# Two transpose banks in a two-layer transformer trunk: one allocation per task in place of alternating halves

## The chip, the core and the metric

The kernel runs on one core of one Trainium2 chip. The metric is the device time of one launch in microseconds (us). TensorE (PE) does the matrix products and the transposes, its weight load is listed apart (PEld), VectorE (DVE), ScalarE (ACT) and GpSimd (POOL) do the elementwise work, SyncE (SP) issues the weight transfers.

## The reference

The input x is (1, 256, 1024) in float32: 256 tokens of 1024 features. Two layers follow each other, each with a half-weighted SwiGLU block, a mixing block and a second half-weighted SwiGLU block:

```python
x = x + 0.5 * swiglu(rms_norm(x, norm_ffn1), w_gate, w_up, w_down)
xn = rms_norm(x, norm_mix)
q, k, v = split(xn @ w_in)                  # 16 heads of 64
x = x + concat(heads_1, heads_2) @ w_out
x = x + 0.5 * swiglu(rms_norm(x, norm_ffn2), w_gate, w_up, w_down)
```

In layer 0 eight heads are stick-breaking heads (a weight per key from log-sigmoids and a running sum over later keys) and eight are block-sparse heads, which with 256 tokens and blocks of 256 are plain causal softmax heads; their q and k get an RMS norm and a rotary embedding. In layer 1 eight heads are forgetting heads (causal softmax whose logits get a difference of cumulated log gates; q and k normed) and eight are dilated-window heads (softmax with fixed weights per distance; q and k normed and rotated).

## The kernel before

**Precision and weights.** Every large product is made of three matmuls with split operands (`mm3`, L153-156): hi by hi, hi by lo, lo by hi. The weights come from HBM through the SP queue into `raw` (3 buffers); ACT casts the hi part (L238), DVE subtracts to get the lo part (L239), 9 buffers for each. Tokens lie in two tiles t of 128. A product is either token-major (`token_major`, weights as the moving operand, 512 columns) or feature-major (`feature_major`, SwiGLU), eight contraction tiles each.

**PSUM.** Eight banks: three `acc` for projections, one `o` for attention outputs, two `z` for logits and for the up projection, and two banks `tt` (one tile of [128, 2, 512]) for transposes. `slot()` (L147) hands out the left and the right 256 columns of both `tt` banks in turn, so two users of `tt` that follow each other lie in different columns of the same two banks. Users of a slot: the transposes of the normed x (`Normed.transpose`, one per token tile and column half of 512), the product `ones x diag` that spreads 1/rms over the partitions (`inverse`), the transposes of the SwiGLU hidden tiles (`hidden`), those of normed or rotated q and k (`project_norm`), the small products of the forget gates (`forget`), the running sums of stick-breaking (`stick_b`, one per head) and the transposes of the softmax weights (`soft_b`, one per head).

**Order of the work.** The order of TensorE is written by the program itself: `Weave` (L70) keeps an estimated clock `pe.t`. A task (a generator) yields a lead; it is resumed, and its next TensorE instructions are put into the stream, at the first poll after that much estimated matmul time. The leads stand at the top: `LEAD_R0` 14 for the rotated q of the first group, `LEAD_R` 9 for its k, `LEAD_N` 6.5 for normed q and k without rotation, `LEAD_F` for the forget gates, `PACE` for the distance between the steps of a head group. The other engines' orders are made by a scheduler from the same program; each engine works through its own queue in that order.

**The mixing block.** The projections come in the order q2, k2, v2 (first group: causal softmax heads in layer 0, dilated heads in layer 1), then in layer 1 the forget gates, then q1, k1, v1 (second group: stick-breaking heads in layer 0, forgetting heads in layer 1), then the output rows of the first group (`out_rows`, 48 matmuls) and those of the second. A group has four pairs of heads. `Group.run` (L581) goes through steps i: `a_(i)` makes the logits of pair i in the two `z` banks and starts its softmax on ACT and DVE (or the log-sigmoids); `b_` transposes the weights of pair i-1 (or makes its running sums), and DVE (or, for stick, ACT through an exponential) brings them to `pT`; `c(i-2)` multiplies by v into `o`; after every second pair `out` splits `o` into `oh` and `ol`. Between the steps TensorE works on what the projections and output rows have left. The second group starts when the first has made four steps.

For rotated heads (`project_norm`) the chain between the projection and its transposes runs over ACT (squares), DVE (`hss`, mean), POOL (power -0.5, `rp`), DVE (`qn`, `qs`), and POOL also makes the products of gains and rotation tables `gc` and `gs` in between.

Of the kernel before, what the change touches and what calls it, by code (L numbers as in the profile page):

```python
# [8 lines left out]
F32 = mybir.dt.float32  # L9
# [7 lines left out]
P = 128  # L17
TAIL = 3
LEAD_R, LEAD_R0, LEAD_N, LEAD_F, OVER = 9.0, 14.0, 6.5, 8.0, 4
LEAD_X = ((1.7, 1.7), (1.7, 3.0))  # L20
LEAD_0 = 3.0
PACE = ((6.5, 6.0), (6.5, 6.0))
# [90 lines left out]
def trunk(ctx, tc, a, out):  # L113
# [30 lines left out]
    tt = psum.tile([P, 2, 512], F32, tag="tt", bufs=1, name="tt")  # L144
    slots = [0]

    def slot():  # L147

        slots[0] += 1
        c0 = (slots[0] % 2) * 256  # L150
        return tt[:, :, c0:c0 + 256]
# [11 lines left out]
    def transposes(src, n):  # L163

        tb = slot()
        for j in range(n):
            for b in range(2):
                r = slice(b * HP, (b + 1) * HP)
                nc.tensor.transpose(tb[:, b, j * HP:(j + 1) * HP], src[r, j * P:(j + 1) * P], ident[r, r])  # L169
            pe.t += 0.06  # L170
        return tb[:, :, :n * HP].rearrange("p b (c t) -> p c b t", t=HP)
# [87 lines left out]
    class Normed:  # L259
# [8 lines left out]
        def start(self, t, h, ps=None, scale=1.0, lead=None, gain=None):  # L268
            self.ready[t].append(pe.spawn(self.transpose(t, h, ps, scale, lead or LEAD_X[t][h], gain)))

        def transpose(self, t, h, ps, scale, lead, gain):
            tk, sl, kk = slice(t * P, (t + 1) * P), slice(h * 512, (h + 1) * 512), slice(4 * h, 4 * h + 4)
            if ps is not None:
                residual(ps, t, h, scale)
            xg = xpool.tile([P, 512], F32, tag="xg", bufs=2, name=nm("xg"))
            nc.vector.tensor_mul(xg, x[t][:, sl], self.g[:, sl] if gain is None else gain)
            self.xg[t].append(xg)
            yield lead
            split_evac(transposes(xg, 4), self.hi[:, kk, tk], self.lo[:, kk, tk])
            if h == 1:  # L280
                self.rdone[t] = pe.spawn(self.inverse(t, self.xg[t]))

        def inverse(self, t, junk):
            sq = small.tile([P, 2], F32, tag="sq", name=nm("sq"))
            for h in range(2):
                nc.scalar.activation(junk[h], x[t][:, h * 512:(h + 1) * 512], AF.Square, accum_out=sq[:, h:h + 1])
            ss = small.tile([P, 1], F32, tag="ss", name=nm("ss"))
            nc.vector.tensor_add(ss, sq[:, 0:1], sq[:, 1:2])
            self.r[t] = rpow(ss, D, 1)
            if self.rb is None:  # L290
                return
            diag = xpool.tile([P, P], F32, tag="diag", name=nm("diag"))
            nc.gpsimd.tensor_mul(diag, ident, self.r[t].to_broadcast([P, P]))
            yield 5.0
            tb = slot()[:, 0]
            mm(tb[:, :P], ones, diag, True)
            nc.scalar.copy(self.rb[:, t * P:(t + 1) * P], tb[:, :P])
# [65 lines left out]
    def ffn(layer, wg, wu, wd, xt, done, between=None):  # L363
        with tc.tile_pool(name=nm("ffn"), bufs=1) as fp:
# [19 lines left out]
            def hidden(hs, c0, n):  # L384
                ft, m = c0 // P, n // P
                vs = [transposes(h, m) for h in hs]
                for t, v in enumerate(vs):
                    split_evac(v, hh[:, ft:ft + m, t * P:(t + 1) * P], hl[:, ft:ft + m, t * P:(t + 1) * P])
# [54 lines left out]
    def _mix(mp, layer, xt, gains, done):  # L443
# [24 lines left out]
        def project_norm(c0, g, tag, lead=LEAD_R):  # L468
# [4 lines left out]
            def norm(t, ps):  # L473
# [8 lines left out]
                if rope:  # L482
# [6 lines left out]
                    yield lead  # L489
# [3 lines left out]
                nc.scalar.activation(halves(qT[:, :, t * P:(t + 1) * P]), transposes(o, 4), AF.Copy,  # L493
# [5 lines left out]
        def forget():  # L499
# [13 lines left out]
            ps = slot()[:, 0]  # L513
# [5 lines left out]
            def rest():  # L519
# [9 lines left out]
                tb = slot()[:, 0]  # L529
# [5 lines left out]
                tb = slot()[:, 0]  # L535
# [24 lines left out]
        class Group:  # L560
# [11 lines left out]
            def run(self, after, pace, other):  # L572
# [5 lines left out]
                for i in range(4 + 2):  # L578
                    if i < 4:
                        a_(i)  # L580
                    if 0 <= i - 1 < 4:  # L581
                        b_(2 * (i - 1))
                        b_(2 * (i - 1) + 1)
# [35 lines left out]
            def stick_b(self, h):  # L619
                sp, ls = self.z.pop(h)  # L620
                b = slot()
                mm(b[:, 0], cv("suf"), sp[:, 0:256], True)
                mm(b[:, 0, P:], cv("nones"), sp[:, 256:384], False)
                mm(b[:, 1, :P], cv("suf"), sp[:, 256:384], True)
                nc.vector.tensor_add(ls[:, 0:256], ls[:, 0:256], b[:, 0])
                nc.vector.tensor_add(ls[:, 256:], ls[:, 256:], b[:, 1, :P])
                pT = self.pT[h] = new("pT", 384, 4)
                nc.scalar.activation(pT, ls, AF.Exp)
# [37 lines left out]
            def soft_b(self, h):  # L666
                tb = transposes(self.z.pop(h), 3)
                pT = self.pT[h] = new("pT", 384, 4)
                nc.vector.tensor_copy(halves(pT.rearrange("p (c t) -> p c t", t=P)), tb)  # L669

            def c(self, p):
# [3 lines left out]
                pTs = [self.pT.pop(2 * p + s) for s in range(2)]  # L675
                for t, (r0, r1) in enumerate(((0, 256), (256, 384))):
                    for s in range(2):
                        o = self.ob[s * HD:s * HD + HD, c0 + t * P:c0 + SEQ]
                        mm(o, self.vs[t][:, (2 * p + s) * HD:(2 * p + s + 1) * HD], pTs[s][:, r0:r1],
# [29 lines left out]
        q2, tq = project_norm(cb, gq, "qT", LEAD_R0)  # L709
# [31 lines left out]
    def second_tile():  # L741
        load_x(1)
        for h in range(2):
            xt.start(1, h, lead=LEAD_0)

    for h in range(2):
        xt.start(0, h, gain=gb[h])
# [48 lines left out]
```

## Time and profile before

| what | value |
|---|---|
| median of 3 runs | 1087.64 us (1087.39 to 1088.31) |
| profiled execution, its own time | 1086.83 us |
| its span in the trace | 1085.0 us |
| mean granted TensorE clock | 0.983 |
| instructions | 13584 |
| TensorE matmuls | 5412 |
| moved from HBM | 176.59 MB, 164 GB/s over the span |

The span runs from the first to the last recorded instruction; the profiled execution's own time is 1.8 us longer. "Idle before" in a row is the time that an engine stood still ahead of the row's first instruction, and behind the arrow stands what ended it. The mixing block of layer 0 lies at about 205 to 360 us, that of layer 1 at about 733 to 897 us; the rest is SwiGLU.

### The profile page before, as it was taken

Reading aid. Unit: us, or ns where it says so; the run is one execution under the profiler, and the core shown is the slowest. Engines: PE = TensorE matmul, PEld = TensorE weight load, DVE = VectorE, ACT = ScalarE, POOL = GpSimd, SP = SyncE. Lnnn points to the kernel's source line nnn. Section 1 sums busy time; section 2 is a strip of 40 time slices with the busy share of each in tenths; the row PEclk is TensorE's granted clock in tenths of the full one; section 3 lists DMA queues with packets and bytes.
Section 4 is the critical chain, followed back from the end, with each engine's and each line's share of the span. In section 5 each row is a group of like instructions: output and inputs, shape, how many; then the busy total and the mean of one; then the engine's idle time right before and its main releaser. Section 6 shows DMA issues by size and latency. Waiting matters only on the chain.

```text
span 1085.0 us, 13584 instructions
## 1 busy us (share of the span) xinstructions
PE 1027.7 (95%) x5412; PEld 841.7 (78%) x5412; DVE 611.6 (56%) x825; ACT 497.8 (46%) x682; POOL 76.1 (7%) x91
## 2 busy tenths in 40 slices
PE   5999999898799999999999999998888989999998
PEld 3888988677676788998788899876755767889986
DVE  5554554666756654564475456447667765555541
ACT  6544543454353644453364445335435544544530
POOL 2000000053000000000010000003431000000000
PEclk9999999999999999999999999999999989999999
DMA  9564665452322564565466456534108316454631
GB/s 327 185 210 128 211 229 180 152 178 97 133 101 78 183 216 135 168 241 185 133 224 216 133 170 242 184 131 161 54 17 281 131 57 215 156 169 164 249 118 39
DMA packets 82657, 178.55 MB, mean 165 GB/s; under 512 B 4993, under 2 KB 21665, under 8 KB 82594
## 3 DMA queue, kind: packets, MB, share of 16 engines
q1 hardware_dynamic: 79776, 174.83, 47.2%
q10 hardware_dynamic: 2818, 2.86, 0.8%
q8 instruction: 42, 0.69, 0.3%
q14 instruction: 21, 0.17, 0.0%
HBM read 176.59 MB, written 1.05 MB: 164 GB/s over the span
## 4 chain that ended last, share of the span: by engine, by line
PE 85%; DVE 8%; ACT 2%; issue 2%; POOL 2%; DMA 1%; SPq 0%; DVEq 0%; ACTq 0%
PE acc L155 51%; PE z L155 24%; PE o L155 6%; DVE lo L239 4%; PE tt L169 3%; ACT hi L238 2%; PE tt L155 1%; POOL rp L217 1%; DMA raw<-in_ffn_w_gate 1%; DMA raw<-in_ffn_w_up 1%; DVE pT L669 1%; DVE mx L653 1%; POOL sq L485 1%; DVE qs L487 0%; DVE x L257 0%
## 5 line engine op out<-in xcount | busy, mean ns | idle before, releaser
L239 DVE TENSOR_TENSOR lo<-raw,hi 128x1024 fp32r<-128x1024 f32 (+1 forms) x344 | 403.0, 1182 | 263.8 <-ACT hi L238 255.7
L238 ACT CAST hi<-raw 128x1024 fp32r<-128x1024 f32 (+1 forms) x344 | 344.1, 1010 | 307.5 <-PE z L155 134.1
L155 PE MATMUL acc<-hi,xt 128*128 128x512 f32 (+1 forms) x1088 | 349.1, 391 | 1.8 <-ACT hi L238 1.8
L155 PEld LDWEIGHTS acc<-hi,xt 128*128 128x128 f32 x1088 | 208.3, 193 | 40.0 <-ACT hi L238 2.2
L155 PE MATMUL z<-hi,xt 128*128 128x512 f32 (+1 forms) x768 | 226.5, 371 | 0.0
L155 PE MATMUL acc<-lo,xt 128*128 128x512 f32 (+1 forms) x544 | 210.0, 386 | 0.9 <-DVE lo L239 0.9
L155 PEld LDWEIGHTS z<-hi,xt 128*128 128x128 f32 x768 | 142.5, 188 | 20.0
L155 PE MATMUL z<-lo,xt 128*128 128x512 f32 (+1 forms) x384 | 142.4, 371 | 0.0
L155 PEld LDWEIGHTS acc<-lo,xt 128*128 128x128 f32 x544 | 105.0, 193 | 17.5 <-DVE lo L239 1.8
L155 PE MATMUL acc<-hi,hh 128*128 128x512 f32 x264 | 105.3, 399 | 0.0
L155 PE MATMUL acc<-lo,hh 128*128 128x512 f32 x264 | 104.5, 396 | 0.0
L155 PE MATMUL acc<-hi,hl 128*128 128x512 f32 x264 | 104.2, 395 | 0.0
L155 PEld LDWEIGHTS z<-lo,xt 128*128 128x128 f32 x384 | 72.1, 188 | 9.9
L217 POOL TENSOR_TENSOR rp<-ms,mhalf 128x1 f32<-128x1 f32 (+1 forms) x24 | 30.3, 1261 | 698.0 <-DVE ms L215 692.7
L380 DVE TENSOR_TENSOR h<-z,sg 128x512 f32<-128x512 f32 (+1 forms) x48 | 30.9, 643 | 55.4 <-PE z L155 55.4
L155 PEld LDWEIGHTS acc<-hi,hh 128*128 128x128 f32 x264 | 49.6, 188 | 11.9
L155 PEld LDWEIGHTS acc<-hi,hl 128*128 128x128 f32 x264 | 49.6, 188 | 11.8
L155 PEld LDWEIGHTS acc<-lo,hh 128*128 128x128 f32 x264 | 49.6, 188 | 11.5
L376 ACT ACTIVATE sg<-acc,rp 128x512 f32<-128x512 f32 (+1 forms) x48 | 31.4, 654 | 42.6 <-PE acc L155 42.0
L251 ACT CAST hh<-tt 128x512 fp32r<-128x512 f32 (+1 forms) x48 | 26.5, 551 | 45.5 <-PE tt L169 25.3
L251 ACT CAST xt<-tt 128x512 fp32r<-128x512 f32 x24 | 14.0, 584 | 63.4 <-PE tt L169 62.7
L252 DVE TENSOR_TENSOR hl<-tt,hh 128x512 fp32r<-128x512 f32 (+1 forms) x48 | 31.0, 646 | 20.3 <-ACT hh L251 19.5
(140 smaller groups left out, 840.5 us busy)
## 6 DMA issues: line engine op xcount, KB each, us to landing
raw<-in_ffn_w_down SPq DMA_DIRECT2D x44, 1024.0 KB
raw<-in_ffn_w_up SPq DMA_DIRECT2D x32, 1024.0 KB
raw<-in_ffn_w_gate SPq DMA_DIRECT2D x30, 1024.0 KB
raw<-in_ffn_w_gate SPq DMA_DIRECT2D x16, 768.0 KB
raw<-in_ffn_w_up SPq DMA_DIRECT2D x16, 768.0 KB
raw<-in_w_in_ab SPq DMA_DIRECT2D x12, 1024.0 KB
raw<-in_w_in_cd SPq DMA_DIRECT2D x12, 1024.0 KB
raw<-in_w_out SPq DMA_DIRECT2D x8, 1024.0 KB
```

What stands on the lines that cost most here:

```text
L155: nc.tensor.matmul(o, lhsT, rhs, start=start, stop=stop, skip_group_check=True)
L169: nc.tensor.transpose(tb[:, b, j * HP:(j + 1) * HP], src[r, j * P:(j + 1) * P], ident[r, r])
L217: nc.gpsimd.tensor_tensor(r, m, mhalf[:, :width], op=ALU.pow)
L238: nc.scalar.copy(hi, wi)
L239: nc.vector.tensor_sub(lo, wi, hi.bitcast(F32))
L251: nc.scalar.copy(halves(hi), v)
L252: nc.vector.tensor_sub(halves(lo), v, halves(hi).bitcast(F32))
L376: nc.scalar.activation(sg[t][:, :n], pg[:, :n], AF.Silu, scale=xt.r[t])
L380: nc.vector.tensor_mul(hs[t][:, :n], pu[:, :n], sg[t][:, :n])
L485: half_swap(lambda u, v: nc.gpsimd.tensor_mul(heads(sw)[:, :, u], heads(qn)[:, :, v], over_heads(gs[:, t, u])))
L653: nc.vector.tensor_reduce(m[:, i:i + 1], z[:, r], axis=AX.X, op=ALU.max, negate=True)
L669: nc.vector.tensor_copy(halves(pT.rearrange("p (c t) -> p c t", t=P)), tb)
```

## The change

`slot()` goes; `pair()` allocates a whole `tt` tile (both banks, all 512 columns) for each task, and the pool has one buffer of it, so the next task waits until the last reader of the tile is done. `transposes` takes several sources and puts them side by side in one such tile. With that:

- `soft_b` and `stick_b` treat both heads of a pair in one task. In `soft_b` the copy of head 0 runs on DVE, that of head 1 on ACT (before, both on DVE): 12 copies move to ACT. In `stick_b` head s has bank s, and one addition of 384 columns takes the place of one of 256 and one of 128. `pT` is one tile of 768 columns per pair, 2 buffers (before 384 per head, 4 buffers).
- `hidden` transposes both token tiles' hidden rows in one allocation.
- At the start, `both` transposes both column halves of x of a token tile in one task. The later norms keep one task per half.
- The `ones x diag` product and the three small products of the forget gates use an `acc` bank.
- `LEAD_R` 9 becomes 14 (which q2 had already), `LEAD_N` 6.5 becomes 10, the first group's pace 6.5 becomes 6.0, and a transposed column block counts 0.065 in `pe.t` in place of 0.06.

```diff
 TAIL = 3
-LEAD_R, LEAD_R0, LEAD_N, LEAD_F, OVER = 9.0, 14.0, 6.5, 8.0, 4
+LEAD_R, LEAD_N, LEAD_F, OVER = 14.0, 10.0, 8.0, 4
 LEAD_X = ((1.7, 1.7), (1.7, 3.0))
 LEAD_0 = 3.0
-PACE = ((6.5, 6.0), (6.5, 6.0))
+PACE = ((6.0, 6.0), (6.0, 6.0))
 HP = P // 2
...
-    tt = psum.tile([P, 2, 512], F32, tag="tt", bufs=1, name="tt")
-    slots = [0]
-    def slot():
-        slots[0] += 1
-        c0 = (slots[0] % 2) * 256
-        return tt[:, :, c0:c0 + 256]
+    def pair():
+        return psum.tile([P, 2, 512], F32, tag="tt", bufs=1, name=nm("tt"))
...
-    def transposes(src, n):
-        tb = slot()
-        for j in range(n):
-            for b in range(2):
-                r = slice(b * HP, (b + 1) * HP)
-                nc.tensor.transpose(tb[:, b, j * HP:(j + 1) * HP], src[r, j * P:(j + 1) * P], ident[r, r])
-            pe.t += 0.06
-        return tb[:, :, :n * HP].rearrange("p b (c t) -> p c b t", t=HP)
+    def transposes(*srcs):
+        tb, n, vs = pair(), 0, []
+        for src in srcs:
+            n0 = n
+            for j in range(src.shape[-1] // P):
+                for b in range(2):
+                    r = slice(b * HP, (b + 1) * HP)
+                    nc.tensor.transpose(tb[:, b, n * HP:(n + 1) * HP], src[r, j * P:(j + 1) * P], ident[r, r])
+                n += 1
+                pe.t += 0.065
+            vs.append(tb[:, :, n0 * HP:n * HP].rearrange("p b (c t) -> p c b t", t=HP))
+        return vs
...
-        def start(self, t, h, ps=None, scale=1.0, lead=None, gain=None):
-            self.ready[t].append(pe.spawn(self.transpose(t, h, ps, scale, lead or LEAD_X[t][h], gain)))
-        def transpose(self, t, h, ps, scale, lead, gain):
+        def start(self, t, h, ps, scale):
+            self.ready[t].append(pe.spawn(self.transpose(t, h, ps, scale, LEAD_X[t][h])))
+        def transpose(self, t, h, ps, scale, lead):
             tk, sl, kk = slice(t * P, (t + 1) * P), slice(h * 512, (h + 1) * 512), slice(4 * h, 4 * h + 4)
-            if ps is not None:
-                residual(ps, t, h, scale)
+            residual(ps, t, h, scale)
             xg = xpool.tile([P, 512], F32, tag="xg", bufs=2, name=nm("xg"))
-            nc.vector.tensor_mul(xg, x[t][:, sl], self.g[:, sl] if gain is None else gain)
+            nc.vector.tensor_mul(xg, x[t][:, sl], self.g[:, sl])
             self.xg[t].append(xg)
             yield lead
-            split_evac(transposes(xg, 4), self.hi[:, kk, tk], self.lo[:, kk, tk])
+            split_evac(*transposes(xg), self.hi[:, kk, tk], self.lo[:, kk, tk])
             if h == 1:
                 self.rdone[t] = pe.spawn(self.inverse(t, self.xg[t]))
+        def both(self, t, gains, lead):
+            self.ready[t].append(pe.spawn(self.transpose_both(t, gains, lead)))
+        def transpose_both(self, t, gains, lead):
+            for h in range(2):
+                xg = xpool.tile([P, 512], F32, tag="xg", bufs=2, name=nm("xg"))
+                nc.vector.tensor_mul(xg, x[t][:, h * 512:(h + 1) * 512], gains[h])
+                self.xg[t].append(xg)
+            yield lead
+            tk = slice(t * P, (t + 1) * P)
+            for h, v in enumerate(transposes(*self.xg[t])):
+                split_evac(v, self.hi[:, 4 * h:4 * h + 4, tk], self.lo[:, 4 * h:4 * h + 4, tk])
+            self.rdone[t] = pe.spawn(self.inverse(t, self.xg[t]))
...
             yield 5.0
-            tb = slot()[:, 0]
+            tb = acc()
             mm(tb[:, :P], ones, diag, True)
...
                 ft, m = c0 // P, n // P
-                vs = [transposes(h, m) for h in hs]
-                for t, v in enumerate(vs):
+                for t, v in enumerate(transposes(*[h[:, :n] for h in hs])):
                     split_evac(v, hh[:, ft:ft + m, t * P:(t + 1) * P], hl[:, ft:ft + m, t * P:(t + 1) * P])
...
-        def project_norm(c0, g, tag, lead=LEAD_R):
+        def project_norm(c0, g, tag):
             qT = mp.tile([P, 4, SEQ], F32, tag=tag, bufs=2, name=nm(tag))
...
                     nc.vector.tensor_add(o, o, sw)
-                    yield lead
+                    yield LEAD_R
                 else:
                     yield LEAD_N
-                nc.scalar.activation(halves(qT[:, :, t * P:(t + 1) * P]), transposes(o, 4), AF.Copy,
+                nc.scalar.activation(halves(qT[:, :, t * P:(t + 1) * P]), transposes(o)[0], AF.Copy,
                                      scale=1.0 if rope else g)
...
             pe.join(*xt.rdone)
-            ps = slot()[:, 0]
+            ps = acc()
             for k in range(KT):
...
                 yield LEAD_F
-                tb = slot()[:, 0]
+                tb = acc()
                 for t in range(2):
                 yield 1.0
-                tb = slot()[:, 0]
+                tb = acc()
                 mm(tb[:8, 0:P], lg[:, 0], cv("le"), True)
...
                     if 0 <= i - 1 < 4:
-                        b_(2 * (i - 1))
-                        b_(2 * (i - 1) + 1)
+                        b_(i - 1)
                     if 0 <= i - 2 < 4:
...
-            def stick_b(self, h):
-                sp, ls = self.z.pop(h)
-                b = slot()
-                mm(b[:, 0], cv("suf"), sp[:, 0:256], True)
-                mm(b[:, 0, P:], cv("nones"), sp[:, 256:384], False)
-                mm(b[:, 1, :P], cv("suf"), sp[:, 256:384], True)
-                nc.vector.tensor_add(ls[:, 0:256], ls[:, 0:256], b[:, 0])
-                nc.vector.tensor_add(ls[:, 256:], ls[:, 256:], b[:, 1, :P])
-                pT = self.pT[h] = new("pT", 384, 4)
-                nc.scalar.activation(pT, ls, AF.Exp)
+            def stick_b(self, p):
+                b = pair()
+                parts = [self.z.pop(2 * p + s) for s in range(2)]
+                for s, (sp, ls) in enumerate(parts):
+                    mm(b[:, s, 0:256], cv("suf"), sp[:, 0:256], True)
+                    mm(b[:, s, 128:256], cv("nones"), sp[:, 256:384], False)
+                    mm(b[:, s, 256:384], cv("suf"), sp[:, 256:384], False)
+                self.pT[p] = new("pT", 768, 2)
+                for s, (sp, ls) in enumerate(parts):
+                    nc.vector.tensor_add(ls, ls, b[:, s, :384])
+                    nc.scalar.activation(self.pT[p][:, s * 384:(s + 1) * 384], ls, AF.Exp)
...
-            def soft_b(self, h):
-                tb = transposes(self.z.pop(h), 3)
-                pT = self.pT[h] = new("pT", 384, 4)
-                nc.vector.tensor_copy(halves(pT.rearrange("p (c t) -> p c t", t=P)), tb)
+            def soft_b(self, p):
+                vs = transposes(*[self.z.pop(2 * p + s) for s in range(2)])
+                self.pT[p] = new("pT", 768, 2)
+                for s, v in enumerate(vs):
+                    pT = self.pT[p][:, s * 384:(s + 1) * 384].rearrange("p (c t) -> p c t", t=P)
+                    (nc.vector.tensor_copy, nc.scalar.copy)[s](halves(pT), v)
                 c0 = (p % 2) * SEQ
-                pTs = [self.pT.pop(2 * p + s) for s in range(2)]
+                pT = self.pT.pop(p)
                 for t, (r0, r1) in enumerate(((0, 256), (256, 384))):
                         o = self.ob[s * HD:s * HD + HD, c0 + t * P:c0 + SEQ]
-                        mm(o, self.vs[t][:, (2 * p + s) * HD:(2 * p + s + 1) * HD], pTs[s][:, r0:r1],
+                        mm(o, self.vs[t][:, (2 * p + s) * HD:(2 * p + s + 1) * HD], pT[:, s * 384 + r0:s * 384 + r1],
                            t == 0 and p % 2 == 0, at_once=2)
...
         gq, gk = gains[0]
-        q2, tq = project_norm(cb, gq, "qT", LEAD_R0)
+        q2, tq = project_norm(cb, gq, "qT")
         k2, tk = project_norm(D + cb, gk, "kT")
...
         load_x(1)
-        for h in range(2):
-            xt.start(1, h, lead=LEAD_0)
-    for h in range(2):
-        xt.start(0, h, gain=gb[h])
+        xt.both(1, [g0[:, h * 512:(h + 1) * 512] for h in range(2)], LEAD_0)
+    xt.both(0, gb, LEAD_X[0][0])
     first_units.extend([lambda: None, second_tile])
```

## The prediction

> **What bounds the kernel now.** The page comes first: span, busy time of TensorE, and the chain of work that ended last.
>
> ```profile
> span 1085.0 us, 13584 instructions
> PE 1027.7 (95%) x5412; PEld 841.7 (78%) x5412; DVE 611.6 (56%) x825; ACT 497.8 (46%) x682; POOL 76.1 (7%) x91
> PE 85%; DVE 8%; ACT 2%; issue 2%; POOL 2%; DMA 1%; SPq 0%; DVEq 0%; ACTq 0%
> ```
>
> TensorE is the bound, busy for 1027.7 of 1085.0 us. The edit takes no matmul away, so it can only win TensorE's idle time (57.3 us) and time that its matmuls lose at a lower clock. The waits of TensorE, summed by what ended them, come next (total, times, longest):
>
> ```profile
> PE tt L169 <- DVE pT L669: 17.5, 12, 2.7
> PE tt L169 <- DVE xt L252: 11.2, 5, 5.7
> PE tt L169 <- DVE ms L215: 6.9, 2, 3.9
> PE tt L155 <- DVE xt L252: 6.7, 2, 3.3
> PE tt L155 <- DVE ls L626: 3.7, 4, 1.6
> PE tt L169 <- ACT qT L493: 1.3, 1, 1.3
> PE tt L169 <- DVE cl L543: 0.6, 1, 0.6
> PE tt L169 <- DVE t L663: 0.4, 1, 0.4
> PE acc L155 <- ACT hi L238: 1.8, 1, 1.8
> PE acc L155 <- DVE lo L239: 0.9, 2, 0.5
> ```
>
> Nearly all of these waits are for the two `tt` banks, and the largest, 12 times for `pT`, is one per pair of soft heads. The timeline shows what such a wait is, first the `ones x diag` product of layer 0:
>
> ```profile
> 209.24 0.40 PE L155 MATMUL o<-lo,hh 128*128 128x512 f32 x1
> 209.47 0.39 PE L155 MATMUL o<-hi,hl 128*128 128x512 f32 x1
> 213.21 0.46 PE L155 MATMUL tt<-diag,ones 128*128 128x128 f32 x2 [3.34 <-DVE xt L252]
> ...
> 214.80 1.05 PE L155 MATMUL acc<-hi,xt 128*128 128x512 f32 x2
> 215.65 0.63 PE L155 MATMUL acc<-lo,xt 128*128 128x512 f32 x1
> ```
>
> The product needs nothing from `xt`; it waits because the evacuation of the other columns of its banks is not over. Behind it matmuls of 512 columns start 0.425 us apart (214.80 to 215.65 is two), ahead of it 0.23 (209.24 to 209.47). The table by stretches gives the granted clock there (PEclk, last but two):
>
> ```profile
> 214.50:217.90 3.40, 3.40 (x10) 2.63 (x9) 1.43 (x2) 0.04 (x1) 0.00 (x0) 0.50 0.85 266
> 248.60:252.00 3.40, 3.40 (x10) 2.63 (x9) 1.44 (x2) 1.04 (x3) 2.47 (x3) 0.51 0.01 2
> 296.40:299.80 3.40, 3.40 (x18) 1.95 (x18) 1.12 (x2) 0.00 (x0) 0.00 (x0) 0.50 1.03 372
> 740.10:743.50 3.40, 3.40 (x10) 2.63 (x9) 2.16 (x2) 0.93 (x2) 0.96 (x1) 0.51 0.91 326
> 774.40:777.80 3.40, 3.40 (x9) 2.62 (x9) 1.69 (x3) 0.69 (x1) 2.19 (x3) 0.51 0.14 54
> 873.30:880.10 6.80, 5.56 (x32) 3.76 (x32) 3.01 (x8) 0.73 (x2) 0.00 (x0) 0.50 0.01 3
> ```
>
> So a stall is paid twice: a stretch of 3.4 us at half clock follows it, with 8 matmuls at 0.425 in place of 0.23, a loss of 8 x 0.195 = 1.5 us (estimate).
>
> **Part by part**, against the profiled execution's 1086.83 us.
>
> *Start.* The second half of each x tile waits until the first half's columns are evacuated:
>
> ```profile
> 16.25 0.57 PE L169 MATMUL tt<-ident,xg 64*128 64x64 f32 x8 [0.28 <-DVE xt L252]
> 20.00 0.69 PE L169 MATMUL tt<-ident,xg 64*128 64x64 f32 x8 [3.18 <-DVE xt L252]
> 20.62 0.79 PE L155 MATMUL acc<-hi,xt 128*128 128x512 f32 x1
> ```
>
> With both halves in one tile the 3.18 goes; the matmuls behind it need token tile 0 only. Bounds 1 (evacuation of tile 0 holds tile 1's task) to 3.4; I take **-3.2**.
>
> *Diag.* On an `acc` bank the product waits for POOL's diag alone, yielded 5 us earlier. Both waits (3.34 each, 6.7 in the row) go: **-6.7**. The acc banks turn over every few matmuls; a wait for one would cost under 1 us each.
>
> *Rotated k2.* Its token tile 0 is the 6.9 row, two true waits for late data.
>
> ```profile
> 243.28 0.46 PE L169 MATMUL tt<-ident,qs 64*128 64x64 f32 x8
> 247.62 0.46 PE L169 MATMUL tt<-ident,qs 64*128 64x64 f32 x8 [3.88 <-DVE ms L215]
> ```
>
> The chain of waits has ahead of the second of these:
>
> ```profile
> 241.53 1.61 POOL rp L217
> ```
>
> This is POOL's power, behind which DVE finishes k2. On TensorE, layer 0, the second tile of q2 and the first of k2 stand side by side before:
>
> ```order
> L155 MATMUL acc_1901<-lo_1898,xt_109 128x512
> L155 MATMUL acc_1901<-hi_1897,xt_110 128x512
> L169 MATMUL tt<-ident,qs_1803 128x64 x8
> L169 MATMUL tt<-ident,qs_1844 128x64 x8
> L155 MATMUL acc_1901<-hi_1897,xt_109 128x512
> ```
>
> After, the same k2 tile (`qs_1857`) is here, in the next projection's accumulation:
>
> ```order
> L150 MATMUL acc_1968<-hi_1911,xt_108 128x512
> L150 MATMUL acc_1968<-lo_1912,xt_108 128x512
> L150 MATMUL acc_1968<-hi_1911,xt_109 128x512
> L166 MATMUL tt_1990<-ident,qs_1857 128x64 x8
> L150 MATMUL acc_1968<-hi_1911,xt_108 128x512
> ```
>
> There are 24 matmuls between the two transposes now: 24 x 0.23 = 5.5 us, against a wait of 3.88, so 1.6 us of slack as long as POOL's and DVE's chain starts from the projection, as the chain of waits shows. In layer 1 (3.0, the rest of the row: 6.9 - 3.9) the order is the same. Bounds 0 to -6.9; I take **-6.5**.
>
> *Clock.* Of the quoted half-clock stretches, 214.5, 248.6, 740.1 and 774.4 each follow one of these four waits; without a stall ahead, 4 x 1.5 = **-6.0** (bounds 0 to -7). The others follow soft pairs or the block's end, where new waits come: no credit.
>
> *Soft pairs.* One of the longer of the twelve waits:
>
> ```profile
> 293.15 0.40 PE L169 MATMUL tt<-ident,t 64*128 64x64 f32 x6
> ...
> 294.24 1.21 DVE L239 TENSOR_TENSOR lo<-raw,hi 128x1024 fp32r<-128x1024 f32 x1
> 295.38 0.55 DVE L669 COPY pT<-tt 128x384 f32<-128x384 f32 x1
> ...
> 295.98 0.40 PE L169 MATMUL tt<-ident,t 64*128 64x64 f32 x6 [2.43 <-DVE pT L669]
> ```
>
> Head 1's transposes wait for head 0's copy, and that stands behind a weight's lo part on DVE. With one tile for both heads this wait has no cause: **-17.5**, all twelve. What comes in its place is that both copies must be over before the next user of `tt` and before `c`. On ACT, layer 0, third pair, before:
>
> ```order
> L659 ACTIVATE t_8_2338,l_2337<-z_2319,mx_2336 128x256
> L686 CAST oh_2366<-o_2266 128x512
> L238 CAST hi_2622<-raw_2616 128x1024
> L238 CAST hi_2661<-raw_2659 128x1024
> L238 CAST hi_2665<-raw_2659 128x1024
> ```
>
> After:
>
> ```order
> L671 ACTIVATE t_7_2375,l_2374<-z_2365,mx_2373 128x128
> L671 ACTIVATE t_8_2385,l_2384<-z_2366,mx_2383 128x128
> L237 CAST hi_2678<-raw_2672 128x1024
> L683 COPY pT_2406<-tt_2393 128x384
> L237 CAST hi_2781<-raw_2779 128x1024
> L671 ACTIVATE t_7_2375,l_2374<-z_2365,mx_2373 128x256
> L671 ACTIVATE t_8_2385,l_2384<-z_2366,mx_2383 128x256
> ```
>
> `t_7`, `t_8` are the fourth pair's exponentials: two casts and a copy that itself waits for DVE now stand in the middle of that softmax, so its transposes come late. A cast and a copy more (about 1.2 + 0.55, by the rows at 294.24 and 295.38) against what little TensorE has left there: between 0 and 4, I take **+2**. In layer 1 the waits for `qT`, `cl` and `t` (2.3 in the rows) may go, but normed q's transposes follow a pair's directly and wait for both its copies (twice 0.55, each perhaps behind a part of 1.2): -2.3 to +4, I take **+1**.
>
> A rule can be judged from the 2.43: columns that nobody reads wait, since the bank is being read. The Trainium skill, "PSUM — Partial Sum Buffer", section "PSUM bank collisions raise a hardware error", says that two engines must not be in one bank and partition quadrant at once, reads included. This speaks against the change: a pair's two heads lie in both banks, so ACT's copy can't run beside DVE's, and ACT's queue stands meanwhile; by it a pair's evacuation would last 1.1 us, without it 0.55: 6.6 us over twelve pairs if nothing hid it (estimate). The trace agrees as far as TensorE against DVE goes.
>
> *Stick pairs.* The four waits for the additions (3.7) go the same way; a late `pT` may cost 0.2: **-3.5**.
>
> *End of layer 1's block* is the largest new cost. On TensorE, before, twelve matmuls of the output rows (`acc_6981`) stand between the second pair's `c` and the fourth pair's logits:
>
> ```order
> L169 MATMUL tt<-ident,t_28_6865 128x64 x6
> L155 MATMUL o_6975<-pT_6879,v_4_6748 64x256
> L155 MATMUL o_6975<-pT_6887,v_4_6748 64x256
> L155 MATMUL o_6975<-pT_6879,v_4_6816 64x128
> L155 MATMUL o_6975<-pT_6887,v_4_6816 64x128
> L155 MATMUL acc_6981<-hi_6906,oh_6592 128x512
> ```
>
> After, the logits (`z_7041`) follow at once, because the output rows were used up a step earlier:
>
> ```order
> L166 MATMUL tt_7020<-ident,t_28_6940 128x64 x6
> L150 MATMUL o_7036<-pT_6961,v_4_6793 64x256 x2
> L150 MATMUL o_7036<-pT_6961,v_4_6830 64x128 x2
> L150 LDWEIGHTS identb
> L150 MATMUL z_7041<-negb,identb 128x2x128
> ```
>
> From there to the second group's output rows TensorE has only links of the softmax chain, whose lengths the trace gives for the fourth pair:
>
> ```profile
> 868.81 0.43 PE L155 MATMUL z<-ck,cq 64*128 64x256 f32 x4
> 871.61 0.40 PE L169 MATMUL tt<-ident,t 64*128 64x64 f32 x6 [2.17 <-DVE pT L669]
> 872.40 0.46 ACT L659 ACTIVATE t<-z,mx 128x256 f32<-128x256 f32 x1
> 873.16 0.74 PE L169 MATMUL tt<-ident,t 64*128 64x64 f32 x6 [0.35 <-DVE t L663]
> 874.08 0.54 DVE L663 TENSOR_SCALAR t<-t,l 128x128 f32<-128x128 f32 x2
> 875.15 0.58 PE L169 MATMUL tt<-ident,t 64*128 64x64 f32 x6 [1.24 <-DVE pT L669]
> ```
>
> The logits end at 869.2, the last exponential that reads their banks at 872.9 (3.7 later), the weights are normed at 874.6 (5.4 later). Now the fourth pair's logits wait 3.7 for the third's banks, with `b` and `c` of about 0.8 each beside it: 2.1 exposed. The third pair's transposes wait 5.4 - 3.7 - 1.4: 0.3. The fourth's wait 5.4 less 1.7 of `b` and `c`: up to 3.7, of which head 0's part (873.2 - 869.2 = 4.0) is earlier, say 2.8. Its copies: 0.7. Sum 5.9, against 0.35 before that isn't counted already: +5.5, and half a stretch more at half clock, 1.5. I take **+7** (2 to 10).
>
> *No cost:* `hidden` (two users before, one now, in the same two banks), the larger first-group pace, the weights (an ACT queue held up by copies delays casts, but TensorE waits for weights only 1.8 + 0.9 us now, and I leave these as they are). A cast that came late would cost its 1 to 1.2 us.
>
> Sum: -3.2 - 6.7 - 6.5 - 6.0 - 17.5 + 2 + 1 - 3.5 + 7 = -33.4, so 1053.4. The median of the runs shown, 1087.64, is 0.8 above the profiled time: 1054.2. I round to **1055**.
>
> A second rule concerns the clock. In the row at 295.98 a wait of 2.43 us was enough for the half-clock stretch at 296.40, and at 873.3 waits of 2.17, 0.35 and 1.24. The Trainium skill, "TensorE: Matmul & The Clock Gate", section "Why this matters for your kernels", wants no idle gap over about 3 us, so by it stalls as short as the new ones would cost no clock and the sum would be 1.5 lower. The trace disagrees, and the measurement decides.
>
> **Rivals.**
>
> *A: the copies become the wait.* Both copies of a pair stand in queues among casts and lo parts (1.2 each), so `c` or the next `tt` user waits for them. For: the ACT order above, and `pT` late by 1.2 in the row at 294.24. Against: a pair's `c` comes a step later. If half of the pairs lose 0.55 + 1.2, six times 1.75 is +10.5: about **1065**.
>
> *B: the rotated data is late all the same.* The prefix is 4.8 us per layer shorter on TensorE (3.34 + 1.5); if the chain hangs on POOL's `gc` and `gs` rather than on the projection, the slack of 1.6 becomes a wait of 3.2, and the clock falls behind it: 2 x 3.2 + 2 x 1.5 = +9.4: about **1064**. With A, 1074.
>
> *C: the edit doesn't free the banks.* If users of `tt` still wait for each other as long, since a whole tile is held until its last reader, pT's 17.5 returns as waits of the next user: about **1073**.
>
> *D: slower.* Steps of the head groups slide behind their filler. A step without filler exposes about 5 us (5.9 over the last two here, 3.7 and more for one). The gains of 43 are eaten when eight of the sixteen steps lie bare and the clock falls with them, 8 x 5 + 2 x 1.5. The place would be the second group of each layer, whose start waits for longer leads of q1 and k1. Against: the order shows bare steps only at the end of layer 1. About **1092**.
>
> **How the numbers follow.** Forecast 0.62 (its own terms: 1045 to 1063), A 0.12, B 0.10, C 0.08, D 0.05, A with B 0.03. The low end 1044 has the largest gains with small new costs; the high end 1072 takes in A and B and leaves out C's upper half, D and A with B, and as much below: about 2 in 10. A measurement of this kernel can tell 0.2% (2.2 us) from no change. Faster by more: all but D and a part of C, 0.93; within: 0.02; slower: 0.05.
>
> **What would show it.** Right: in the waits of TensorE after, the row `tt <- pT` under 4 us and no `tt <- xt` but the first; no half-clock stretch behind the diag products and k2; new waits of `z` and `tt` in the last steps of layer 1's block, 5 us or more together. Wrong: waits of `o` for `pT` on ACT (A), of `qs` transposes for `ms` again (B), of `tt` for ACT's `pT` (C), or idle TensorE in the middle of layer 1's second group (D).

## The result and the profile after

The changed kernel takes 1050.61 us (median of 4 runs, 1047.35 to 1051.28) against 1087.91 us of the kernel before in the same session. The ratio is 0.9651, with an interval of 0.9631 to 0.9672: 37 us less. The profiled execution takes 1051.01 us, 35.8 less than the profiled 1086.83 of before; the prediction's sum was -33.4, its forecast 1055 us. The page and the waits of TensorE come first. In the rows every product stands at the line of the helper `mm` (L155 before, L150 after), every transpose at L169 or L166; in the kernel before, `mm3` is L158 to 161, `Weave` L78 and `Group.run` L572.

```profile
span 1049.2 us, 13558 instructions
PE 1019.5 (97%) x5412; PEld 837.8 (80%) x5412; DVE 604.4 (58%) x805; ACT 503.2 (48%) x694; POOL 81.6 (8%) x91
PE 87%; DVE 5%; issue 2%; ACT 2%; DMA 2%; POOL 1%; SPq 0%; ACTq 0%; POOLq 0%; DVEq 0%
```

```profile
PE tt L166 <- ACT pT L683: 5.1, 2, 3.9
PE acc L150 <- ACT xt L250: 3.9, 1, 3.9
PE z L150 <- ACT t L671: 3.9, 4, 2.3
PE tt L166 <- DVE t L675: 2.4, 3, 1.0
PE acc L150 <- DMA grow<-in_norm_ffn: 2.2, 1, 2.2
PE tt L166 <- DVE xt L251: 2.1, 2, 1.0
PE acc L150 <- ACT hi L237: 1.8, 1, 1.8
PE acc L150 <- DVE lo L238: 1.7, 1, 1.7
PE tt L166 <- DVE xg L288: 1.0, 1, 1.0
PE z L150 <- ACT kT L505: 0.8, 1, 0.8
PE tt L166 <- DVE ms L214: 0.5, 1, 0.5
```

The same 5412 matmuls are busy for 8.2 us less (1027.7 to 1019.5). About 4.5 of it is the clock in layer 0 (worked out further down); where the other 3.7 went is not shown. The rest of the gain is waiting. The twelve waits for `pT` on DVE (17.5), the diag product's (6.7), the stick additions' (3.7) are gone, and the two of k2 (6.9) as well: the `ms` row that is left (0.5) stands at the start of the kernel. What came is in the first and third row: a copy on ACT, and the `z` banks.

By stage, from the starts of the same instructions in both traces: the start gives 3.4 us; the diag waits 3.5 each; layer 0's block behind its diag product shrinks from 147.6 to 128.8 us (18.8), layer 1's from 157.8 to 151.2 (6.6); the SwiGLU stretches are equal within 0.1. The sum is 35.8.

Layer 0's diag product on TensorE now follows the SwiGLU at once, and matmuls behind it start 0.23 us apart:

```profile
206.07 0.39 PE L150 MATMUL o<-hi,hl 128*128 128x512 f32 x1
206.30 0.38 PE L150 MATMUL acc<-diag,ones 128*128 128x128 f32 x2
206.44 0.47 PE L150 MATMUL acc<-hi,xt 128*128 128x512 f32 x1
206.75 0.39 PE L150 MATMUL acc<-lo,xt 128*128 128x512 f32 x1
206.98 0.63 PE L150 MATMUL acc<-hi,xt 128*128 128x512 f32 x2
```

Layer 1 is where new waits lie. Three engines at 776 us, from the timeline:

```profile
776.35 0.55 DVE L683 COPY pT<-tt 128x384 f32<-128x384 f32 x1
...
777.37 1.99 ACT L237 CAST hi<-raw 128x1024 fp32r<-128x1024 f32 x2 [1.34 <-DMA raw<-in_w_in_cd]
...
779.63 0.47 ACT L683 COPY pT<-tt 128x384 f32<-128x384 f32 x1
...
780.15 0.69 PE L166 MATMUL tt<-ident,qn 64*128 64x64 f32 x8 [3.94 <-ACT pT L683]
```

Head 0's copy is done by DVE at 776.9, head 1's by ACT only at 780.1, behind two casts that themselves waited for a weight to arrive. The normed q's transposes need the banks and wait 3.94 us. At the end of the block:

```profile
833.12 0.55 DVE L683 COPY pT<-tt 128x384 f32<-128x384 f32 x1
...
833.80 0.48 ACT L683 COPY pT<-tt 128x384 f32<-128x384 f32 x1
...
834.79 0.27 PE L150 MATMUL z<-negb,identb 128*128 128x256 bf16 x1 [2.31 <-ACT t L671]
```

The fourth pair's logits wait 2.31 us for the third's exponentials, as worked out (2.1). The two copies of a pair come one after the other in all twelve pairs, and in four of them ACT stands idle until DVE's copy is over (0.99 to 3.10 us), as in the last pair:

```profile
841.46 0.48 ACT L683 COPY pT<-tt 128x384 f32<-128x384 f32 x1 [1.44 <-DVE pT L683]
```

The Trainium skill's rule of one engine in a bank ("PSUM — Partial Sum Buffer", "PSUM bank collisions raise a hardware error") asks for this order; the trace agrees.

### The profile page after: what moved, and what is told of

It is laid out like the page before. It is cut to its first block, busy times and chain, and to the rows that moved or that the text cites. A ratio compares the mean times of both kernels' runs of the same rounds, so it can differ in the third digit from the quotient of the medians.

```text
span 1049.2 us, 13558 instructions
## 1 busy us (share of the span) xinstructions
PE 1019.5 (97%) x5412; PEld 837.8 (80%) x5412; DVE 604.4 (58%) x805; ACT 503.2 (48%) x694; POOL 81.6 (8%) x91
## 3 DMA queue, kind: packets, MB, share of 16 engines
HBM read 176.59 MB, written 1.05 MB: 169 GB/s over the span
## 4 chain that ended last, share of the span: by engine, by line
PE 87%; DVE 5%; issue 2%; ACT 2%; DMA 2%; POOL 1%; SPq 0%; ACTq 0%; POOLq 0%; DVEq 0%
PE acc L150 52%; PE z L150 24%; PE o L150 7%; PE tt L166 3%; DVE lo L238 2%; ACT hi L237 1%; DMA raw<-in_w_in_cd 1%; PE tt L150 1%; DMA hg<-in_g_q_b 1%; POOL sq L497 1%; POOL rp L216 1%; DVE qn L492 0%; SPq L565 0%; DVE t L675 0%; ACT t L671 0%
## 5 line engine op out<-in xcount | busy, mean ns | idle before, releaser
L150 PE MATMUL acc<-hi,xt 128*128 128x512 f32 (+1 forms) x1088 | 345.8, 388 | 5.7 <-ACT xt L250 3.9
L150 PEld LDWEIGHTS acc<-hi,xt 128*128 128x128 f32 x1088 | 206.0, 191 | 43.6 <-ACT xt L250 4.1
L150 PE MATMUL z<-hi,xt 128*128 128x512 f32 (+1 forms) x768 | 226.4, 371 | 0.0
L150 PE MATMUL acc<-lo,xt 128*128 128x512 f32 (+1 forms) x544 | 208.2, 383 | 1.7 <-DVE lo L238 1.7
L150 PEld LDWEIGHTS z<-hi,xt 128*128 128x128 f32 x768 | 142.4, 188 | 20.0
L150 PE MATMUL z<-lo,xt 128*128 128x512 f32 (+1 forms) x384 | 142.3, 371 | 0.0
L150 PEld LDWEIGHTS acc<-lo,xt 128*128 128x128 f32 x544 | 104.1, 191 | 17.4 <-DVE lo L238 2.0
L150 PE MATMUL acc<-hi,hh 128*128 128x512 f32 x264 | 105.2, 399 | 0.0
L150 PE MATMUL acc<-lo,hh 128*128 128x512 f32 x264 | 104.5, 396 | 0.0
L150 PE MATMUL acc<-hi,hl 128*128 128x512 f32 x264 | 104.2, 395 | 0.0
L150 PEld LDWEIGHTS z<-lo,xt 128*128 128x128 f32 x384 | 72.1, 188 | 9.9
L150 PEld LDWEIGHTS acc<-hi,hh 128*128 128x128 f32 x264 | 49.6, 188 | 11.9
L150 PEld LDWEIGHTS acc<-hi,hl 128*128 128x128 f32 x264 | 49.6, 188 | 11.8
L150 PEld LDWEIGHTS acc<-lo,hh 128*128 128x128 f32 x264 | 49.6, 188 | 11.5
L251 DVE TENSOR_TENSOR hl<-tt,hh 128x512 fp32r<-128x512 f32 (+1 forms) x48 | 31.0, 646 | 20.3 <-ACT hh L250 19.5
```

Of the source, the lines that this page charges most:

```text
L150: nc.tensor.matmul(o, lhsT, rhs, start=start, stop=stop, skip_group_check=True)
L251: nc.vector.tensor_sub(halves(lo), v, halves(hi).bitcast(F32))
```

## The experiments

All times are medians, each with the ratio to the kernel before in its own session; the change itself has 1050.61 and 0.9651.

**e1_per_head.** In the changed kernel:

```diff
-                vs = transposes(*[self.z.pop(2 * p + s) for s in range(2)])
+                    v = transposes(self.z.pop(2 * p + s))[0]
-                    (nc.vector.tensor_copy, nc.scalar.copy)[s](halves(pT), v)
+                    nc.vector.tensor_copy(halves(pT), v)
```

> The changed kernel with the softmax pairs undone: each head's transposes take a whole allocation of the two banks and both copies run on DVE; all else of the change stays. Theory (head 1's transposes wait for head 0's copy because both lie in the same banks): the twelve waits for pT come back, 15 to 19 us, and 2 to 4 us of half clock with them, so 1066 to 1073 us. Rival (the leads and the diag product made the gain, and pairs would be hidden by the new order): 1050 to 1056 us.

Measured 1063.26 us, 0.978 (0.9759 to 0.9802): 12.7 more than the change. Its waits of TensorE have the row back:

```profile
PE tt L166 <- DVE pT L683: 19.5, 13, 3.6
```

The mechanism stands, but the time is 2.7 below the expected 1066: the row returns with 19.5, and the change's own waits for ACT's `pT` (5.1) and for `t` in the `z` banks (3.9) go. So the pairs are worth 17.5 gross and about 13 net. The edit also takes the second copy from ACT back to DVE; that this is not what costs the time is seen in e5 below, which does it alone and takes as long as the change.

**e2_k2_lead.** k2's lead 14 back to 9.5 (q2 keeps 14).

> The changed kernel with k2's lead at 9.5 in place of 14 (q2 keeps 14), so that only three matmuls stand between q2's second tile and k2's first. Theory (k2's rotated data is late whatever the banks do): waits of the k2 transposes for DVE's ms of about 3.2 us in layer 0 and 2.3 us in layer 1 return, with a half-clock stretch of 1.5 us behind each, so 1057 to 1060 us. Rival (the wait was only an after-effect of the diag stall on POOL's and DVE's chain): 1050 to 1053 us.

Measured 1057.93 us, 0.9725 (0.9701 to 0.975): 7.3 more than the change and within the expected 1057 to 1060. Its row:

```profile
PE tt L166 <- DVE ms L214: 3.8, 3, 2.8
```

In layer 0 k2 waits 2.80 us with half clock behind it, so the data is late whatever the banks do. In layer 1 the wait is only 0.41; yet about half of the 7.3 us lies there, in other waits (ACT's casts 5.0 in all, in place of 1.8). The theory holds for layer 0; for layer 1 the time agrees and the reason doesn't.

**e3_diag_alone.** The kernel before with `tb = acc()` for the diag product.

> The kernel before with one edit: the product of ones and diag takes an acc bank. Theory: the two waits of 3.34 us go, and the half clock behind them (1.5 us each), so 9.7 us less: 1077 to 1080 us. Rival (the wait only moves, to the k2 transposes, since POOL's chain keeps its time): the k2 waits grow from 3.9 and 3.0 us to about 7 each and the time is 1085 to 1088 us.

Measured 1080.74 us, 0.9938 (0.9916 to 0.9959): 4.5 to 9.1 less by the interval, against the 9.7 of the theory; the median lies 0.7 above its 1077 to 1080. Both diag waits are gone and the k2 waits didn't grow (3.69 and 1.30), so the rival doesn't hold. In layer 1 the scheduler put a weight's parts between two heads' normalisations on DVE, and the third pair waits 1.64 + 5.00 there (1.32 + 2.65 before); but k2 waits 1.7 less and the half clock is 3.4 us shorter, so that layer 1's block behind its diag product is 1.8 us shorter all the same. What is missing is in layer 0, whose block got 2.6 us longer (150.1 in place of 147.6), with half clock for 17.1 us of it in place of 10.2. The same wait of 2.69 us on TensorE, in the kernel before and in this one:

```profile
277.19 0.40 PE L169 MATMUL tt<-ident,t 64*128 64x64 f32 x6 [2.69 <-DVE pT L669]
...
278.79 0.40 PE L155 MATMUL acc<-xt,hi 128*128 128x256 f32 x2
```

```profile
273.86 0.58 PE L169 MATMUL tt<-ident,t 64*128 64x64 f32 x6 [2.69 <-DVE pT L669]
...
276.66 0.63 PE L155 MATMUL acc<-xt,hi 128*128 128x256 f32 x2
```

Before, it cost no clock; here, 0.63 in place of 0.40 for two matmuls, and the table by stretches has half clock for two times 3.4 us:

```profile
273.20:280.00 6.80, 6.14 (x33) 5.32 (x34) 3.09 (x11) 1.83 (x8) 0.00 (x0) 0.50 0.44 166
```

What a stall of this length costs in clock depends on when it falls, and the traces show how. Count windows of 3.41 us, the length of the shortest whole stretch at half clock, forward and back from the start of such a stretch, and add up TensorE's idle time in each. In the fourteen traces of this case, from 30 us on, a full-clock window with more than 1.7 us of idle time is always followed by one at half clock, and one with less than 1.3 us never is; between the two both occur (1.36 to 1.64). The wait of 2.69 us is split between two windows in the kernel before (1.44 and 1.25 us of idle time) and puts 2.07 us into one here. So it is the sum in a window that counts and not the single gap, and a gain early in the program can be given back at a later stall that hasn't changed. The Trainium skill, "TensorE: Matmul & The Clock Gate", section "What's actually happening", has the clock decided in free-running windows of 3413 ns; the stretches of 3.4 and 6.8 us in these traces agree.

**e4_junk_in_gap.** The kernel before; the added products leave the output's values as they were.

```diff
             yield 5.0
+            if t == 0:
+                junk = acc()
+                for i in range(13):
+                    nc.tensor.matmul(junk, identb, identb.unsqueeze(1).to_broadcast([P, 4, P]), start=i == 0,
+                                     stop=i == 12, skip_group_check=True)
             tb = slot()[:, 0]
```

> The kernel before with 13 products of a constant by itself (bf16, 512 columns, into a free acc bank, never read) put ahead of token tile 0's diag product in both layers: work that fills the 3.34 us wait and shortens nothing. Theory (idle time of TensorE costs the clock of the stretch behind it): no half clock behind the two diag products, 2 x 1.5 us less: 1084 to 1086 us in spite of 26 more matmuls. Rival (the clock falls there for another reason, or the added work delays the product): 1087.5 to 1091 us.

Measured 1089.19 us, 1.0014 (1.0001 to 1.0028): by the time alone, a miss. The place itself shows the theory, in the timeline and the stretch behind:

```profile
209.88 2.98 PE L298 MATMUL acc<-identb 128*128 128x512 bf16 x13
213.38 0.46 PE L155 MATMUL tt<-diag,ones 128*128 128x128 f32 x2 [0.52 <-DVE xt L252]
```

```profile
213.40:217.00 3.60, 3.60 (x17) 3.02 (x18) 2.79 (x3) 1.21 (x2) 0.00 (x0) 1.00 1.02 332
```

Full clock, and from the diag product to k2's first transposes 32.8 us (34.4 before), in layer 1 31.9 (33.5): 1.6 each, as expected. The 3.2 us are lost again by the two things of e3: the same 1.65 + 5.00 in layer 1, and half clock in layer 0, for 6.8 us behind k2 where there were 3.4 and for 6.8 us from 276.0 where there was none. So idle time does cost the clock, and the total is no measure of one place.

**e5, e6, e7: three attempts on layer 1's new waits.** Each changes one line of the changed kernel: both copies on DVE (e5); `LEAD_N` 10 to 6.5 (e6); the second pace of layer 1 6.0 to 5.0 (e7).

> The changed kernel with both copies of a softmax pair on DVE (head 1's is on ACT in the change). TensorE's order is the same. Theory (ACT's copy is late because it stands behind exponentials and a weight's cast in ACT's queue, and the normed q's transposes wait for it): the waits of TensorE for ACT's pT (3.9 and 1.2 us in layer 1) fall to about 1.5 together, the 1.25 us wait of layer 0's fourth pair goes: 4 to 6 us less than the change, 1044 to 1047 us. Rival (DVE's queue with its lo parts makes the second copy as late or later): 1050 to 1054 us, with waits for DVE's pT in their place.

> The changed kernel with LEAD_N at 6.5 in place of 10: normed q's transposes stand ahead of the second dilated pair, 19 instructions away from it, not behind its products. Theory (the longer lead put them directly behind a pair, where they wait for its two copies): the waits for ACT's pT (5.1 us) go, waits of 0.5 to 1.5 us for the norm's data come: 2 to 5 us less, 1046 to 1049 us. Rival (the norm's data is late at the shorter lead, as k2's was): waits for the norm of 3 us and more, 1051 to 1056 us.

> The changed kernel with layer 1's second group at a pace of 5.0 in place of 6.0: six output-row matmuls stand between the second pair's products and the fourth pair's logits, where none stood. Theory (the bare end of layer 1's block costs 2.3 us of waiting for the z banks): that wait falls by six matmuls, 1.4 us, and the earlier steps wait no more than now: 1 to 2 us less, 1048.5 to 1050 us. Rival (the steps come too early for their softmax and wait there): waits for t or z in the first steps, 1051 to 1054 us.

Measured 1051.68 (0.9655, 0.9641 to 0.9669), 1051.16 (0.9651, 0.9637 to 0.9665) and 1050.92 us (0.9644, 0.963 to 0.9657): no difference from the change, three times. Each wait aimed at shrank or went, and another took its place. The largest row of e5, e6 and e7:

```profile
PE tt L166 <- DVE t L675: 5.2, 3, 4.0
```

```profile
PE tt L166 <- DVE t L675: 8.9, 2, 5.6
```

```profile
PE tt L166 <- ACT pT L683: 5.9, 2, 5.1
```

All three theories of the time fall. TensorE's gaps of 0.25 us and more in layer 1's block add up to 14.1 in the change and 17.4, 15.1 and 15.3 here: so something else may hold the block. SP's queue in the change shows a candidate:

```profile
739.50 0.37 SPq L231 DMA_DIRECT2D raw<-in_w_in_cd  x1
766.83 5.13 SPq L565 DMA_DIRECT2D rows<-cl  x8
772.06 2.47 SPq L231 DMA_DIRECT2D raw<-in_w_in_cd  x3
```

No weight is issued for 32 us. The transfers that spread the forget gates stand ahead of k1's and v1's weights, and `cl` and `rows` lie in the three weight buffers `raw`. The kernel before has the same hole (770.45 to 810.89 us).

**e8_rows_off_sp, e9_cl_own_buffer, e11_pool_queue_only.** In `forget` of the changed kernel, e8 makes both edits, e9 the first, e11 the second:

```diff
-                cl = raw_p.tile([8, 4, SEQ], F32, tag="raw", name="cl")
+                cl = mp.tile([8, 4, SEQ], F32, name="cl")
-                            nc.sync.dma_start(rows[b0 + 2 * i + j:b0 + 2 * i + j + 1, i],
+                            nc.gpsimd.dma_start(rows[b0 + 2 * i + j:b0 + 2 * i + j + 1, i],
```

> The changed kernel with the forget gates' eight small transfers (rows from cl) issued by POOL instead of SP, and cl in a buffer of its own instead of one of the three weight buffers. Theory (what holds layer 1's block is one thing, which moves when a lead or a copy moves: SP's queue stands from 739.5 to 766.8 us behind these transfers, so k1's and v1's weights are 27 us late, and ACT's queue with the copies of the pairs behind them): the waits for weights (1.8 and 1.7 us) and ACT's pT (3.9 and 1.2 us) fall to under 3 us together: 4 to 7 us less than the change, 1043.5 to 1047 us. Rival (the block is held by the softmax chain itself, on DVE and ACT): the waits move again and the time is 1049 to 1052 us.

> The changed kernel with cl in a buffer of its own, the eight transfers still in SP's queue. Theory (the queue is what holds, not the number of weight buffers): as the change within 1.5 us, 1049 to 1052 us, with SP's wait for cl of about 27 us as before. Rival (the buffer holds): 1044 to 1048 us.

> The changed kernel with the eight transfers issued by POOL, cl left in one of the three weight buffers. The run with cl in a buffer of its own left the transfers in SP's queue, but the scheduler then put them behind k1's and v1's weights, so queue and buffer were not told apart. Theory (the buffer holds: the next weight that shares cl's and rows' buffers can't be loaded until they are read, whatever queue issues): the weights behind are late still, 1048 to 1052 us, with waits for them or for ACT's pT of 5 us or more. Rival (the queue holds): 1043 to 1046 us, as with both.

Measured: e8 1044.58 us, 0.9594 (0.9572 to 0.9616); e9 1044.10, 0.9592 (0.9571 to 0.9613); e11 1054.58, 0.9685 (0.9663 to 0.9707). The late weights do hold a part of the block: in e8 the waits for them are gone, ACT's `pT` costs 1.9 in place of 5.1, and the gaps of 14.1 fall to 9.4. The buffer alone is enough to keep them late: e11 has a free queue and no gain, 4.0 us more than the change and 2.6 above its range. e9's theory falls too, but e9 doesn't clear the queue, since with `cl` in its own buffer the scheduler also put the transfers behind three of the weights (764.39 us), and SP waits 4.1 us for `cl` in place of 26.9. What the queue would cost by itself is not shown. In e9 SP issues the weights early:

```profile
737.25 12.54 SPq L231 DMA_DIRECT2D raw<-in_w_in_cd  x3
759.78 0.37 SPq L231 DMA_DIRECT2D raw<-in_w_out  x1
```

In e11 SP has only weights to issue, and yet issues none between 739.99 and 770.81 us; the next cast on ACT waits longest of all:

```profile
776.16 1.99 ACT L237 CAST hi<-raw 128x1024 fp32r<-128x1024 f32 x2 [7.76 <-DMA raw<-in_w_in_cd]
```

**e10_off_sp_paces, e12_off_sp_lead_n.** e8 with `LEAD_N` 6.5 and the pace of 5.0 (e10), and with `LEAD_N` 6.5 alone (e12).

> The kernel of the first run of this call, with LEAD_N 6.5 and layer 1's second pace 5.0 as well. Theory (with the weights in time, the shorter lead takes q's transposes away from a pair, and the faster pace keeps filler for the block's end): another 1 to 3 us less than that run, 1041 to 1045 us. Rival (the two change nothing, as by themselves): equal to that run within 1 us.

> cl in its own buffer, transfers by POOL, LEAD_N 6.5, pace 6.0: the run with both leads changed less the pace. Theory (the lead, which takes q's transposes away from a pair, gives most of the 6.8 us): 1038 to 1041 us, with a wait for the z banks of 2.3 us at the end of the block. Rival (the pace gives most): 1042 to 1045 us.

Measured 1037.82 us, 0.9528 (0.9506 to 0.955) and 1037.72 us, 0.9531 (0.951 to 0.9553). Both are below their ranges, e10 by 3.2 us and e12 by 0.3. The lead, worth nothing by itself (e6), gives 6.9 us once the weights are in time; the pace gives nothing beside it. In e12 no wait for ACT's `pT` and none for a weight is left; layer 1's block keeps mainly this row:

```profile
PE tt L166 <- DVE t L675: 6.1, 4, 3.4
```

The block's end has its wait on `t` (3.4), not on the `z` banks as expected. e12 and e10 beat both kernels: 51 us less than before, 13 less than the change. No run takes the start, the stick pairs or the forget gates' `acc` bank alone; what is said of these rests on the traces of the two kernels.

## Why the prediction was right, point by point

- *What bounds*: right. TensorE does the same matmuls, and what could be told apart of the gain is its waits and its clock.
- *Start* (-3.2): right; 3.8 at the matmul behind tile 1's transposes (16.83, was 20.62), 3.4 from 30 us on.
- *Diag* (-6.7): right; 3.5 and 3.5, and e3 by itself.
- *k2* (-6.5): right; no wait is left. e2 brings layer 0's back (2.80), but of layer 1's 3.0 only 0.41, so that this one was late data is not shown. POOL's chain moved with the projection, so rival B didn't come.
- *Clock* (-6.0): the mechanism was right (1.6 per place in e4), its places were not. Layer 0's three stretches are gone, 296.40's too, which got no credit. Layer 0's block won 18.8: 14.4 of waits (3.9 k2, 6.8 pairs, 3.7 stick) less the new 1.25 for `z` (forecast 2), about 4.5 of clock, and 1.1 that isn't told apart. Layer 1 won nothing here: five stretches before and four after, 23.8 us at half clock both times, the latter behind the new waits:

```profile
767.90:774.70 6.80, 5.49 (x18) 3.85 (x20) 3.15 (x4) 2.10 (x3) 2.49 (x1) 0.50 0.22 49
778.20:785.00 6.80, 4.85 (x18) 3.86 (x19) 5.75 (x12) 5.90 (x10) 0.00 (x0) 0.50 0.95 355
798.60:802.00 3.40, 3.40 (x13) 2.31 (x12) 0.52 (x1) 0.96 (x2) 0.00 (x0) 0.50 0.94 297
836.20:843.00 6.80, 6.02 (x52) 4.13 (x50) 4.10 (x13) 3.16 (x11) 0.00 (x0) 0.50 0.00 0
```

- *Soft pairs* (-17.5): right as to the waits, all twelve; e1 puts the net at about 13.
- *Normed q and the forget gates in layer 1* (+1): mis-sized. The waits for `qT`, `cl` and `t` went (2.3), 5.1 us for ACT's `pT` came, with 0.8 more for weights (3.5 against 2.7), 1.8 for the third pair and 0.8 for `kT`: about +6. The step that failed is "each perhaps behind a part of 1.2": ACT stood behind casts that waited for transfers, which I had set aside, since TensorE itself hardly waited for weights. The +1 is the term furthest off.
- *End of layer 1's block* (+7): mis-sized the other way. From the third pair's logits to the second group's output rows the change takes 13.5 us (829.87 to 843.35); before it took 17.05 (861.36 to 878.41) with 2.8 of filler and 4.2 of waits for `pT` in it, which leaves 10.0. So it cost +3.5. The z banks' 2.31 came as worked out; the waits behind (2.8 + 0.7) shrank to 0.7, since TensorE's own links ran at half clock there (the last of the rows above). The 1.5 of clock in the term is a whole stretch by the prediction's own figure, not half of one.
- *The sum*: the misses of about +5 and -3.5 and the 1.5 of clock that didn't come cancel in part, and some gain has no term: 1.1 in layer 0, and in layer 1 about 2.5 (3.0 of k2 and 10.6 of pairs less 6 and 3.5 make 4.1, measured 6.6). That -33.4 came so near to -35.8 is in part luck.
- *Rivals*: A came in one place (two waits, 5.1) and not as six; C and D didn't come: no wait of `tt` for a pair's predecessor, bare steps only at the block's end. D's 1092 doesn't follow from its terms: 1055 and 43 make 1098, or 1091 without the +7 that the block's end has already.
- *Signs named ahead*: the half clock behind the diag products and k2 is gone, as named. The others missed: `tt <- pT` is 5.1 and not under 4, the new waits at the end of layer 1's block are 3.2 (2.31 + 0.19 + 0.66) and not 5, and two waits of `tt` for `xt` (1.03 and 1.05) stay, which the kernel before has too. Waits of `tt` for ACT's `pT` were named as the sign of C and came, but with 5.1 of its 17.5.
- *The gap of about 3 us* (the Trainium skill, "TensorE: Matmul & The Clock Gate", "Why this matters for your kernels"): the last stretch follows gaps of 2.31 us and less, and that of 798.60 gaps of 1.20 us and less, so the trace still disagrees.

## What to carry to other kernels

Two users of one PSUM bank wait for each other's evacuation even without common data: give them one allocation, or move the small one to another bank, and look for the half clock behind each such wait. When a wait is removed and the time stays, add up all waits of the stage: a sum that only changes names can point at one cause upstream, here a small tile in a weight buffer. Once it is gone, try again what failed before (the lead: 0 us alone, 6.9 us after).

## What was not expected of the hardware

The time of a run goes with the clock that was granted in it: in the session of e1 to e4 the kernel before took 1084.8 us at a mean granted clock of 0.986, 1086.6 to 1088.8 at 0.983 to 0.984, and 1090.0 and 1091.0 at 0.978 and 0.980; the change took 1047.35 at 0.994 and 1051.0 to 1051.3 at 0.988. So a spread of 0.4 to 0.6% belongs to one and the same kernel, and an edit of 3 us is seen in the trace of its place better than in the time.
